# Odd chunks at off-diagonal places of TensorE, in a second PSUM bank, in the triangular inverse and solve of a recurrence

## The chip, the core and the metric

One core of a Trainium2 chip runs the whole program. TensorE (PE) multiplies, with its weight loads shown as a row of their own (PEld); VectorE (DVE), ScalarE (ACT) and GpSimd (POOL) work on elements; SyncE (SP) issues the transfers. The metric is the time of one execution on the device, in microseconds, and the lower the better.

## The reference, cut to what matters

The program computes two blocks one after the other: an attention and mixture-of-experts layer, and then a layer with a convolution, a recurrence and gates. Only the recurrence of the second block is touched. For each of 16 heads of width 64 it runs over 528 positions:

```python
def step(s, inp):
    r_t, w_t, k_t, v_t, a_t, b_t = inp
    sa = jnp.einsum("bhvk,bhk->bhv", s, a_t)
    s = s * w_t[:, :, None, :] + sa[..., None] * b_t[:, :, None, :] + v_t[..., None] * k_t[:, :, None, :]
    y = jnp.einsum("bhvk,bhk->bhv", s, r_t)
    return s, y
```

The kernel does this in chunks of 64 positions. Inside a chunk the steps depend on each other through a strictly triangular 64x64 matrix, so each chunk needs the inverse of (identity minus that matrix), applied to a right-hand side.

## The kernel before

The second block treats two heads at a time: `j` runs from 0 to 7, with head `h` (0 or 1) of the pair in partitions 64h to 64h+63. There are 8 full chunks `c`, and one short one at the start that has its own small tiles (`NX0`, `NT0`). Four stages belong to a `j`: `stage_p` projects (dense products of 24 triples, lines 192 to 194), `stage_x` prepares the chunks, inverts and solves, `stage_y` runs the state over the chunks (line 1532), and beside them `conv_tile` does 30 multiply-adds per tile on DVE (line 1593) and `gate_tile` makes gates from dense products of width 258.

Nobody writes the order of the instructions out by hand. `OFF`, `STEP` and `at` give each stage a priority, and a scheduler lays all instructions of an engine into one list, which the engine then works through in order. So the dense products of lines 192 to 194 (`m` tiles) of another `j`, or of a gate, stand between the steps of the inverse on PE, and the multiply-adds of line 1593 stand between them on DVE. A dense weight tile is split first into two halves, `wh` by ACT (line 160) and `wl` by DVE (line 161), and PE waits for both.

The inverse (lines 1422 to 1438) works on the 32x32 blocks on the diagonal, four for each chunk: quarter `q` of the partitions holds one. The tile `NX` has two planes for each chunk: plane 0 is a power N of the block, plane 1 the running sum X. Five steps `st_` double the power: DVE transposes plane 0 into `NT` (line 1424), PE multiplies `NT` with both planes of `NX` (line 1429), so that N becomes N times N and X gains N times X, DVE adds the old X (line 1435) and ACT copies the new power (line 1437). The first step has plane 0 alone, the last plane 1 alone, so their products are 32 columns wide and those of the three middle steps 64. All are f32, which the trace shows as two records for each product, and each stands at TensorE's place (32q, 32q). The results go to a PSUM tile of the pool `x`, which has two buffers of one bank each (`xps`).

The short chunk does the same in `NX0` (line 1448). Lines 1473 and 1483 join the two 32x32 inverses of a head into a 64x64 one (`X64`), and line 1501 multiplies that with the right-hand side `RT`: 16 products of 64x64 by 64x128, at the places (0, 0) for head 0 and (64, 64) for head 1, chunks 0 to 3 in one bank and 4 to 7 in another. ACT and DVE copy each bank to `LL` (lines 1503 and 1504); line 1512 multiplies `LL` with `QQ` for the tiles `GE` that `stage_y` reads. Those products take their PSUM tile from the same two buffers.

The program below prints these functions with the lines of the profile.

Of the kernel before, what the change touches and what calls it, by code (L numbers as in the profile page):

```python
# [14 lines left out]
AF = mybir.ActivationFunctionType  # L15
OP = mybir.AluOpType
# [75 lines left out]
def tile_blocks(ctx: ExitStack, tc: tile.TileContext, a, out, dbg=None):  # L92
# [30 lines left out]
    x = a["x"][0]  # L123
# [989 lines left out]
    def xps():  # L1113
        return pxy.tile([128, 512], F32, name="x", tag="x", bufs=2)
# [102 lines left out]
    def c4(t):  # L1217
        return t.rearrange("p (c t) -> p c t", c=4)
# [71 lines left out]
    def stage_x(j, z):  # L1290
# [129 lines left out]
        for st_ in range(5):  # L1420
            first, last = st_ == 0, st_ == 4
            w0_, w1_ = int(last), 1 if first else 2
            NT = c8(S2("NT"))
            V.transpose(NT, NX[:, :, 0])
            p = xps().rearrange("p (c w t) -> p c w t", c=8, w=2)
            for c in range(8):
                for q in range(4):
                    qs = slice(32 * q, 32 * q + 32)
                    TE.matmul(p[qs, c, w0_:w1_], NT[qs, c], NX[qs, c, w0_:w1_], start=True, stop=True,
                              tile_position=(32 * q, 32 * q))  # L1430
            nx = UX("NX", "NX", 512, 3).rearrange("p (c w t) -> p c w t", c=8, w=2)
            if first:
                V.tensor_tensor(nx[:, :, 1], NX[:, :, 0], id32[:, None, :].to_broadcast([128, 8, 32]), op=OP.add)
            else:
                V.tensor_tensor(nx[:, :, 1], p[:, :, 1], NX[:, :, 1], op=OP.add)
            if not last:
                A.activation(nx[:, :, 0], p[:, :, 0], AF.Copy)
            NX = nx
        p0 = xps()
        for st_ in range(4):  # L1440
# [52 lines left out]
                      start=True, stop=True, tile_position=(h * 64, h * 64))  # L1493
        for h in range(2):
            A.activation(WV0[:32, h], p[h * 64:h * 64 + 32, 0:64], AF.Copy)
        for i in range(2):
            p = c4(xps())
            for c in range(4):
                for h in range(2):
                    hs = slice(h * 64, (h + 1) * 64)  # L1500
                    TE.matmul(p[hs, c], X64[hs, 4 * i + c], RT[hs, 4 * i + c], start=True, stop=True,
                              tile_position=(h * 64, h * 64))
            A.activation(LL[0:64, 4 * i:4 * i + 4, 0:128], p[0:64], AF.Copy)
            V.tensor_copy(LL[0:64, 4 * i:4 * i + 4, 128:256], p[64:128])

        GE = z.GE = [UX("GE", "GE", 1024, 4).rearrange("p (c h n) -> p c h n", c=4, h=2) for _ in range(2)]
        for i in range(2):
# [396 lines left out]
```

## Time and profile before

| what | value |
|---|---|
| median of three runs | 2100.97 us (2096.94 to 2103.51) |
| the profiled execution | 2105.41 us, its span 2103.6 us |
| mean granted clock of TensorE | 0.979 |
| busy over the span | PE 94%, PEld 79%, DVE 63%, ACT 40%, POOL 2% |
| the second block's loop over `j` | from about 920 to 1455 us of the span |

The profiled execution was 4.4 us slower than the median of the runs shown. The shares of busy time are means over stages that are bound by different things; what counts for this change is the stretch from 920 to 1455 us. A PE record lasts to its modelled end, some 0.2 to 0.3 us after it started, so records overlap and gaps below that length don't show as idle time; the time that a group of products takes is read from its start to the start of what follows it.

### The profile page before, as it was taken

What the parts mean: (1) busy time and instruction counts of PE and PEld (TensorE: products, weight loads), DVE (VectorE), ACT (ScalarE), POOL (GpSimd) and SP (SyncE); (2) the same over time, 40 slices, a digit from 0 to 9 for tenths busy, and PEclk for the clock granted to TensorE, in tenths of its full rate; (3) what the DMA queues carried; (4) which work ended last, traced back from release to release, by engine and by line L of the source; (5) the groups of instructions that cost most, each with busy time, mean ns of one, the idle gap of its engine ahead of it and who ended that gap; (6) DMA issues with size and microseconds to landing.
All of it is one profiled execution on the core that took longest, in us unless ns stands there. A gap on an engine that the chain in (4) does not pass through costs nothing.

```text
span 2103.6 us, 41384 instructions
## 1 busy us (share of the span) xinstructions
PE 1980.9 (94%) x17133; PEld 1672.3 (79%) x17133; DVE 1320.2 (63%) x2919; ACT 832.3 (40%) x1751; POOL 33.9 (2%) x101
## 2 busy tenths in 40 slices
PE   7999999997898999799999999989899999999998
PEld 7778687886454555699888888878799989899997
DVE  4789835443234333679999889886443476455566
ACT  5443544332101111655655656544433253233333
POOL 0000000000000000100000000000000000000000
PEclk9999999998799999999999999999999999999999
DMA  5212021344897997432121112113543323333331
GB/s 160 56 31 82 21 78 44 100 146 154 313 357 301 356 361 273 57 81 58 41 57 57 56 41 59 52 42 103 150 122 94 109 64 91 95 97 91 91 116 51
DMA packets 236964, 247.38 MB, mean 118 GB/s; under 512 B 32156, under 2 KB 190787, under 8 KB 236771
## 3 DMA queue, kind: packets, MB, share of 16 engines
q1 hardware_dynamic: 233315, 234.19, 34.9%
q0 software_dynamic: 2304, 8.39, 1.1%
q8 instruction: 137, 2.24, 0.4%
q10 hardware_dynamic: 1152, 2.10, 0.3%
q14 instruction: 56, 0.46, 0.1%
HBM read 233.79 MB, written 10.84 MB: 116 GB/s over the span
## 4 chain that ended last, share of the span: by engine, by line
PE 68%; issue 13%; DVE 12%; ACT 4%; DMA 2%; POOL 1%; SPq 0%; DVEq 0%; ACTq 0%; POOLq 0%
PE m L194 10%; PE m L192 10%; PE m L193 10%; PE ps L192 5%; PE ps L193 5%; PE ps L194 5%; DVE cv L1593 3%; PE ps L430 2%; PE q L192 2%; PE q L194 2%; DVE wl L161 2%; PE q L193 2%; PE ps L448 1%; PE ps L887 1%; PE y L1532 1%
## 5 line engine op out<-in xcount | busy, mean ns | idle before, releaser
L192 PE MATMUL m<-hh,wh 128*128 128x258 f32 (+1 forms) x1648 | 468.0, 290 | 7.4 <-ACT wh L160 3.0
L194 PE MATMUL m<-hh,wl 128*128 128x258 f32 (+1 forms) x1648 | 466.8, 290 | 2.1 <-DVE wl L161 2.1
L193 PE MATMUL m<-hl,wh 128*128 128x258 f32 (+1 forms) x1648 | 465.7, 288 | 3.0 <-DVE hl L161 1.7
L161 DVE TENSOR_TENSOR wl<-wr,wh 128x1024 fp32r<-128x1024 f32 (+1 forms) x205 | 248.0, 1212 | 228.4 <-ACT wh L160 227.3
L160 ACT ACTIVATE wh<-wr 128x1024 fp32r<-128x1024 f32 (+1 forms) x205 | 214.9, 1050 | 374.4 <-PE m L193 221.3
L192 PEld LDWEIGHTS m<-hh,wh 128*128 128x128 f32 x1648 | 308.4, 189 | 13.9 <-ACT wh L160 3.9
L193 PEld LDWEIGHTS m<-hl,wh 128*128 128x128 f32 x1648 | 308.8, 190 | 7.2 <-DVE hl L161 2.3
L194 PEld LDWEIGHTS m<-hh,wl 128*128 128x128 f32 x1648 | 307.7, 189 | 7.1 <-DVE wl L161 3.3
L1593 DVE SCALAR_TENSOR_TENSOR cv<-th,vec,cv 128x516 f32<-128x516 f32 (+9 forms) x240 | 176.4, 738 | 2.6
L887 PE MATMUL ps<-we,xg 128*64 128x256 f32 x1024 | 135.6, 397 | 5.8 <-PEq L928 5.8
L887 PEld LDWEIGHTS ps<-we,xg 128*64 128x64 f32 x1024 | 76.4, 142 | 53.9 <-issue 21.8
L192 PE MATMUL ps<-wh,hh 128*128 128x256 f32 x352 | 101.7, 289 | 0.9 <-ACT wh L160 0.9
L193 PE MATMUL ps<-wl,hh 128*128 128x256 f32 x352 | 101.2, 288 | 0.7 <-DVE wl L161 0.7
L194 PE MATMUL ps<-wh,hl 128*128 128x256 f32 x352 | 101.0, 287 | 0.0
L192 PEld LDWEIGHTS ps<-wh,hh 128*128 128x128 f32 x352 | 67.4, 191 | 2.0 <-ACT wh L160 1.3
L193 PEld LDWEIGHTS ps<-wl,hh 128*128 128x128 f32 x352 | 67.5, 192 | 1.5 <-DVE wl L161 1.0
L194 PEld LDWEIGHTS ps<-wh,hl 128*128 128x128 f32 x352 | 67.3, 191 | 0.1
L902 PE MATMUL ps<-we,hT 128*64 128x512 f32 x256 | 60.8, 615 | 3.8 <-ACT hT L154 3.3
L1031 PE MATMUL ps<-yph,oht 128*128 128x512 f32 x128 | 56.9, 445 | 6.6 <-DVE x L1033 3.6
L890 ACT ACTIVATE hd<-ps,cw 128x256 f32<-128x256 f32 x16 | 7.6, 474 | 139.6 <-PE ps L887 139.6
L1800 ACT ACTIVATE uu<-m 128x258 f32<-128x258 f32 x88 | 33.1, 378 | 65.6 <-PE m L194 65.6
L192 PE MATMUL q<-wh,zh 128*128 128x512 f32 x144 | 56.7, 396 | 0.4 <-DVE ac L1865 0.2
(554 smaller groups left out, 4201.6 us busy)
## 6 DMA issues: line engine op xcount, KB each, us to landing
wr<-in_w_in_dram SPq DMA_DIRECT2D x94, 512.0 KB
we<-in_w_gate_dram SPq DMA_DIRECT2D x64, 512.0 KB
we<-in_w_up_dram SPq DMA_DIRECT2D x64, 512.0 KB
we<-in_w_down_dram SPq DMA_DIRECT2D x64, 512.0 KB
wr<-in_ffn_up_dram SPq DMA_DIRECT2D x44, 512.0 KB
wr<-in_ffn_down_dram SPq DMA_DIRECT2D x18, 512.0 KB
wr<-in_w_out_dram SPq DMA_DIRECT2D x8, 512.0 KB
wr<-in_w_rwkv_out_dram SPq DMA_DIRECT2D x8, 512.0 KB
```

Of the source, the lines that this page charges most:

```text
L160: A.activation(h, r, AF.Copy)
L161: V.tensor_tensor(l, r, h, op=OP.subtract)
L192: TE.matmul(o, lh, rh, start=start, stop=False)
L193: TE.matmul(o, lh, rl, start=False, stop=False)
L194: TE.matmul(o, ll, rh, start=False, stop=stop)
L430: TE.matmul(ss[r], qf(j)[:, bi * 128:(bi + 1) * 128], kf(j)[:, :nk], start=True, stop=True)
L448: TE.matmul(po[r * 64:(r + 1) * 64, f * 128:(f + 1) * 128], v(kb)[:, j * 64:(j + 1) * 64], ptbs[r][:, kb * 128:(kb + 1) * 128], start=(kb ...
L887: TE.matmul(pg[s * 64:(s + 1) * 64, c0:c0 + 256], XG[k][:, s * 64:(s + 1) * 64], w[s][k], start=(k == 0), stop=(k == 7))
L902: TE.matmul(py[s * 64:(s + 1) * 64], hT[:, f * 128 + s * 64:f * 128 + (s + 1) * 64], wd[s][f][:, hf * 512:(hf + 1) * 512], start=(f == 0), ...
L1031: TE.matmul(p, oht[:, bs], yp[hf][0], start=(i == 0), stop=False)
L1593: V.scalar_tensor_tensor(cv[:, lo:], th[:, lo - d:N2 - d], cdw[:, f, 30 - d:31 - d], cv[:, lo:], op0=OP.mult, op1=OP.add)
L1800: A.activation(t, q, AF.Copy)
```

## The change

In the inverse, each step takes both buffers of the pool `x`, half a bank of each. Even chunks keep the places (32q, 32q) and write to the first. Odd chunks write to the second, and in all steps but the first they stand at places off the diagonal: in steps 1 and 3 rows 32q with columns 32(q+1), so that the result lies one quarter further on, and in steps 2 and 4 rows 32(q+1) with columns 32q, which brings it back. The old X isn't added by DVE any more: a second product for each block, with a 32x32 identity as weights and plane 1 of `NX` as the moving operand, adds it in PSUM (the new line 1435). Then ACT copies the even chunks and DVE the odd ones (new lines 1446 and 1447). In the first step ACT makes two copies instead of one.

In the solve, chunk 2c+i stands at (64h, 64h) for i = 0 and at (64h, 64(1-h)) for i = 1, in the bank of i; the products of both banks take turns, and the copies to `LL` follow for all even chunks and all odd chunks.

```diff
-            p = xps().rearrange("p (c w t) -> p c w t", c=8, w=2)
-            for c in range(8):
-                for q in range(4):
-                    qs = slice(32 * q, 32 * q + 32)
-                    TE.matmul(p[qs, c, w0_:w1_], NT[qs, c], NX[qs, c, w0_:w1_], start=True, stop=True,
-                              tile_position=(32 * q, 32 * q))
+            p = [xps()[:, :256].rearrange("p (c w t) -> p c w t", c=4, w=2) for _ in range(2)]
+            for c in range(0, 8, 2):
+
+                for one in range(1 if first else 2):
+                    for go in range(2):
+                        for q in range(4):
+                            up_ = 0 if first else go
+                            u, o = (q, (q + up_) % 4) if st_ % 2 else ((q + up_) % 4, q)
+                            us, os_ = slice(32 * u, 32 * u + 32), slice(32 * o, 32 * o + 32)
+                            if one:
+                                TE.matmul(p[go][os_, c // 2, 1], id32[us], NX[us, c + go, 1], start=False, stop=True,
+                                          tile_position=(32 * u, 32 * o), skip_group_check=True)
+                            else:
+                                TE.matmul(p[go][os_, c // 2, w0_:w1_], NT[us, c + go], NX[us, c + go, w0_:w1_],
+                                          start=True, stop=first, tile_position=(32 * u, 32 * o), skip_group_check=True)
...
+                A.activation(nx[:, 0::2, 0], p[0][:, :, 0], AF.Copy)
+                A.activation(nx[:, 1::2, 0], p[1][:, :, 0], AF.Copy)
             else:
-                V.tensor_tensor(nx[:, :, 1], p[:, :, 1], NX[:, :, 1], op=OP.add)
-            if not last:
-                A.activation(nx[:, :, 0], p[:, :, 0], AF.Copy)
+                A.activation(nx[:, 0::2, w0_:], p[0][:, :, w0_:], AF.Copy)
+                V.tensor_copy(nx[:, 1::2, w0_:], p[1][:, :, w0_:])
...
+        p = [c4(xps()) for _ in range(2)]
+        for c in range(4):
+            for i in range(2):
+                for h in range(2):
+                    hs, o = slice(h * 64, (h + 1) * 64), 64 * (h ^ i)
+                    TE.matmul(p[i][o:o + 64, c], X64[hs, 2 * c + i], RT[hs, 2 * c + i], start=True, stop=True,
+                              tile_position=(h * 64, o))
         for i in range(2):
-            p = c4(xps())
-            for c in range(4):
-                for h in range(2):
-                    hs = slice(h * 64, (h + 1) * 64)
-                    TE.matmul(p[hs, c], X64[hs, 4 * i + c], RT[hs, 4 * i + c], start=True, stop=True,
-                              tile_position=(h * 64, h * 64))
-            A.activation(LL[0:64, 4 * i:4 * i + 4, 0:128], p[0:64], AF.Copy)
-            V.tensor_copy(LL[0:64, 4 * i:4 * i + 4, 128:256], p[64:128])
+            L_ = LL[0:64, i::2].rearrange("p c (x n) -> p c x n", x=2)
+            A.activation(L_[:, :, i], p[i][0:64], AF.Copy)
+            V.tensor_copy(L_[:, :, 1 - i], p[i][64:128])
```

The lines behind it move down, by 10 after the inverse and by 13 after the solve (1448 is 1458, 1501 is 1512, 1512 is 1525, 1593 is 1606). The scheduler lays the lists out anew. Three places of them follow, before and after.

PE, the last step of the inverse for `j` = 0 and the short chunk's first product behind it; before:

```order
L194 MATMUL m_9822<-hh,wl 128x264
L1429 MATMUL x<-NX,NT 32x32 x32
L1448 MATMUL x<-NX_9350,NT_9548 32x32 x4
L192 MATMUL m_9822<-hh,wh 128x264
L193 MATMUL m_9822<-hl,wh 128x264
L194 MATMUL m_9822<-hh,wl 128x264
```

The same place after, where L1435 is the product with the identity and L1458 the short chunk:

```order
L1438 MATMUL x<-NX,NT 32x32 x8
L1435 MATMUL x<-NX,cst_90 32x32 x8
L1438 MATMUL x<-NX,NT 32x32 x8
L1435 MATMUL x<-NX,cst_90 32x32 x8
L1438 MATMUL x<-NX,NT 32x32 x8
L1435 MATMUL x<-NX,cst_90 32x32 x8
L1438 MATMUL x<-NX,NT 32x32 x8
L1435 MATMUL x<-NX,cst_90 32x32 x8
L192 MATMUL m_9957<-hh,wh 128x264
L193 MATMUL m_9957<-hl,wh 128x264
L1458 MATMUL x<-NX_9350,NT_9683 32x32 x4
L194 MATMUL m_9957<-hh,wl 128x264
```

The step has twice the products, and the short chunk's, which followed at once, now stand apart behind two dense products.

PE, from the solve to the first products with `LL` for `j` = 2; before:

```order
L1501 MATMUL x<-RT,X_11428 64x128 x15
L192 MATMUL m_11765<-hh,wh 128x264
L193 MATMUL m_11765<-hl,wh 128x264
L194 MATMUL m_11765<-hh,wl 128x264
L192 MATMUL m_11765<-hh,wh 128x264
L193 MATMUL m_11765<-hl,wh 128x264
L194 MATMUL m_11765<-hh,wl 128x264
L192 MATMUL m_11765<-hh,wh 128x264
L193 MATMUL m_11765<-hl,wh 128x264
L194 MATMUL m_11765<-hh,wl 128x264
L192 MATMUL m_11765<-hh,wh 128x264
L1512 MATMUL x<-QQ,LL 128x128 x8
```

The same place after (L1512 is now the solve, L1525 the product with `LL`, L1277 and L1278 are dense products of `stage_p`):

```order
L1512 MATMUL x<-RT,X_11833 64x128 x8
L1278 MATMUL m_12245<-low,lwl 128x264
L1277 MATMUL m_12246<-low,lwh 128x264
L1278 MATMUL m_12246<-low,lwl 128x264
L1277 MATMUL m_12247<-loa,lwh 128x264
L1278 MATMUL m_12247<-loa,lwl 128x264
L1525 MATMUL x<-QQ,LL 128x128
L1277 MATMUL m_12248<-loa,lwh 128x264
L1278 MATMUL m_12248<-loa,lwl 128x264
L1525 MATMUL x<-QQ,LL 128x128 x7
```

Five dense products stand between the solve and the first product with `LL` instead of ten, and that product stands alone.

DVE, the inverse for `j` = 7, the last pair of heads, from the second step's addition to the fourth step's; before:

```order
L1435 TENSOR_TENSOR NX<-x,NX 128x8x32
L1593 SCALAR_TENSOR_TENSOR cv<-th,vec_1326,cv 128x516
L1424 STREAM_TRANSPOSE NT<-NX 128x256
L1593 SCALAR_TENSOR_TENSOR cv<-th,vec_1326,cv 128x516
L161 TENSOR_TENSOR wl<-wr,wh 128x1024
L1435 TENSOR_TENSOR NX<-x,NX 128x8x32
L1593 SCALAR_TENSOR_TENSOR cv<-th,vec_1326,cv 128x516
L1424 STREAM_TRANSPOSE NT<-NX 128x256
L1593 SCALAR_TENSOR_TENSOR cv<-th,vec_1326,cv 128x516
L161 TENSOR_TENSOR wl<-wr,wh 128x1024
L1435 TENSOR_TENSOR NX<-x,NX 128x8x32
L1593 SCALAR_TENSOR_TENSOR cv<-th,vec_1326,cv 128x516
```

The same place after, from ahead of the second step's transpose to behind the third step's (L1606 is the multiply-add of `conv_tile`, L1447 the copy of the odd chunks):

```order
L161 TENSOR_TENSOR wl<-wr,wh 128x1024
L1606 SCALAR_TENSOR_TENSOR cv<-th,vec_1326,cv 128x516 x4
L1424 STREAM_TRANSPOSE NT<-NX 128x256
L1606 SCALAR_TENSOR_TENSOR cv<-th,vec_1326,cv 128x516 x3
L1606 SCALAR_TENSOR_TENSOR cv<-th,vec_1326,cv 128x515
L1447 COPY NX<-x 128x4x64
L1606 SCALAR_TENSOR_TENSOR cv<-th,vec_1326,cv 128x514
L1424 STREAM_TRANSPOSE NT<-NX 128x256
L1606 SCALAR_TENSOR_TENSOR cv<-th,vec_1326,cv 128x513
L1606 SCALAR_TENSOR_TENSOR cv<-th,vec_1326,cv 128x512
L1606 SCALAR_TENSOR_TENSOR cv<-th,vec_1326,cv 128x511
L1606 SCALAR_TENSOR_TENSOR cv<-th,vec_1326,cv 128x510
```

Two splits of gate weights (L161) stand inside this piece before; after, the splits stand ahead of the second step or behind the last, and more multiply-adds stand between the steps. The dense products that need the early ones can stand earlier in PE's list between its steps: by the first step's products 35 of width 258 in place of 8, by the last step's 92 in place of 34.

## Rows read from the trace of the kernel before

**Rows 1.** busy time by stretch; columns as headed; `j` = 1 and 7

```profile
core 0: us, PE busy (x) PEld busy (x) DVE busy (x) ACT busy (x) POOL busy (x), PEclk, DMA share, GB/s
984.00:1048.00 64.00, 63.57 (x918) 57.37 (x917) 58.99 (x128) 37.72 (x90) 1.16 (x7) 1.00 0.20 55
...
1378.00:1440.00 62.00, 53.85 (x817) 47.35 (x815) 55.28 (x120) 28.59 (x68) 0.00 (x0) 0.92 0.10 28
```

**Rows 2.** waits, 920 to 1440 us: total us, times, longest us

```profile
PE x L1429 <- DVE NT L1424: 5.0, 11, 1.5
```

**Rows 3.** timeline of PE, the inverse: start us, duration us; [idle before]

```profile
950.12 1.09 PE L1429 MATMUL x<-NX,NT 32*32 32x64 f32 x64
951.15 0.39 PE L193 MATMUL m<-hl,wh 128*128 128x264 f32 x1
...
956.94 0.74 PE L1429 MATMUL x<-NX,NT 32*32 32x32 f32 x64 [0.16 <-DVE NT L1424]
957.53 0.26 PE L1448 MATMUL x<-NX,NT 32*32 32x32 f32 x8
...
1008.84 0.75 PE L1429 MATMUL x<-NX,NT 32*32 32x32 f32 x64
...
1009.52 0.39 PE L194 MATMUL m<-hh,wl 128*128 128x264 f32 x1
```

**Rows 4.** busy time of line 1429 in slices of two steps

```profile
1009.04:1009.14 0.10, 0.10 (x35) 0.10 (x23) 1.00 0.00 0
950.32:950.52 0.20, 0.20 (x28) 0.20 (x22) 1.00 0.00 0
```

**Rows 5.** timeline of PE: products whose places share columns, or rows

```profile
1383.65 1.16 PE L1346 MATMUL x<-ARI,BK 64*128 64x128 f32 x16
1384.74 0.39 PE L192 MATMUL m<-hh,wh 128*128 128x264 f32 x1
...
1401.94 1.15 PE L1399 MATMUL x<-LL,SA 64*64 64x64 f32 x32
1403.02 0.33 PE L1406 MATMUL x<-WV,SC 32*64 32x64 f32 x4
```

**Rows 6.** timeline: solve and first products with `LL`, `j` = 0

```profile
965.55 1.96 PE L1501 MATMUL x<-RT,X 64*64 64x128 f32 x30
966.67 0.59 ACT L1503 ACTIVATE LL<-x 64x512 f32<-64x512 f32 x1 [1.64 <-PE x L1501]
...
967.30 0.69 DVE L1504 COPY LL<-x 64x512 f32<-64x512 f32 x1 [0.71 <-ACT LL L1503]
...
967.44 0.39 PE L192 MATMUL m<-hh,wh 128*128 128x264 f32 x1
...
968.04 1.16 PE L1512 MATMUL x<-QQ,LL 128*128 128x128 f32 x8
...
968.96 0.37 PE L1278 MATMUL m<-low,lwl 128*128 128x264 f32 x1
```

**Rows 7.** groups, 920 to 1440 us: | busy us, mean ns | idle before

```profile
L1512 PE MATMUL x<-QQ,LL 128*128 128x128 f32 x256 | 34.6, 280 | 0.0
...
L1435 DVE TENSOR_TENSOR NX<-x,NX 128x256 f32<-128x256 f32 x32 | 13.4, 419 | 1.3 <-PE x L1429 1.3
...
L1437 ACT ACTIVATE NX<-x 128x256 f32<-128x256 f32 x32 | 12.2, 380 | 34.2 <-DVE NX L1435 30.4 <-PE x L1429 3.8
```

**Rows 8.** busy time around the inverse of `j` = 7; columns as rows 1

```profile
1390.00:1396.00 6.00, 4.66 (x49) 4.01 (x50) 4.59 (x15) 2.49 (x6) 0.00 (x0) 0.72 0.00 0
1396.00:1402.00 6.00, 4.71 (x30) 2.98 (x29) 4.61 (x13) 2.78 (x8) 0.00 (x0) 1.00 0.12 45
1402.00:1408.00 6.00, 3.96 (x164) 3.40 (x164) 6.00 (x10) 2.46 (x6) 0.00 (x0) 0.86 0.02 5
1408.00:1414.00 6.00, 4.47 (x92) 4.16 (x96) 5.70 (x11) 0.77 (x2) 0.00 (x0) 0.57 0.35 95
```

**Rows 9.** timeline of DVE around the inverse of `j` = 7

```profile
1401.04 4.68 DVE L1593 SCALAR_TENSOR_TENSOR cv<-th,vec,cv 128x503 f32<-128x503 f32 x7
```

## The prediction, made before the run

> **What bounds the kernel now.** I read the busy time by stretch first. For a middle pair of heads PE is busy 63.57 of 64 us, DVE 58.99, ACT 37.72, at full clock; the seven pairs `j` = 0 to 6 look alike, and the last, `j` = 7, leaves PE 8 us of 62 and a clock of 0.92 [rows 1]. So for seven pairs PE bounds, and what counts is the time that a piece of PE's list takes. The list of waits says that the transposes hold up PE 5.0 us in all over the eight inverses, 11 times [rows 2]; the dense products between the steps cover the rest of that chain. The timeline of PE then gives the pieces themselves, from the start of one to the start of what follows. A 64-wide step of the inverse takes 951.15 - 950.12 = 1.03 us, a 32-wide one 1009.52 - 1008.84 = 0.68 us, both with 64 records [rows 3]; the next dense product starts some 0.14 us behind the last record (it does so in both: 0.54 us for 63 records at 8.6 ns, 0.89 at 14 ns). These two rates stand in the slices: about 35 records, each some 0.2 us long, touch a slice of 0.1 us of the 32-wide step, which is 0.3 us / 35 = 8.6 ns apiece; 28 touch 0.2 us of the 64-wide one, 0.4 / 28 = 14 ns [rows 4]. The second is the pace at which four places work; the first may be that too (four places, half the columns), but may as well be the pace at which PE takes instructions. This is the question on which the sum turns.
>
> **What the change does to PE, for each `j`.** Removed are no products; each of the four later steps gets 64 more records, the products with the identity.
>
> (a) The three middle steps. If the even and the odd places work side by side, a step of 128 records lasts as long as it takes to feed them: 127 gaps of 8.6 ns are 1.09 us, and with 0.14 behind it is 1.23 us, against 1.03: +0.20 each, +0.60. I take 8.6 ns because it is the fastest sustained rate of small products that a row shows [rows 4]; the bound below is that places alone set the pace (rival B), the bound above that the places take turns (rival C). That places which share rows or columns work side by side is shown for pairs. One place needs 4 x 14 = 56 ns for a record of 64 columns, so 112 for 128. Line 1399, whose two places share their rows, takes 1403.02 - 1401.94 = 1.08 us for 32 records of 64 columns, (1.08 - 0.14) / 32 = 29 ns each, half of 56; line 1346, whose two places share columns and write to two banks, takes 1.09 us for 16 of 128, (1.09 - 0.14) / 16 = 59 ns, half of 112 [rows 5]. No row shows both kinds at once, as here.
>
> (b) The last step has 128 records where it had 64, 32 wide: 1.23 - 0.68 = +0.55 us. The first step keeps 64 records in the same places: 0.
>
> (c) The solve: 30 of its 32 records take 1.89 us [rows 6], of which 0.14 lies behind them. The other 1.75 us are 58 ns a record of 128 columns, two places at work; with four they become half: -0.87 us. The bound above is 0.
>
> (d) The lists are cut into more pieces. The short chunk's first products followed the last step directly (0.59 us after its start, no gap [rows 3]) and now stand alone, and the first product with `LL` stands apart; every switch between small and dense products costs some 0.1 us (the 0.14 of above is of this kind). Two more in a `j`, less what falls away: +0.15 us (0 to 0.35).
>
> (e) A new wait. In before the short chunk's first product took the other PSUM buffer, which was free. Now the last step holds both, so it waits for ACT's copy of the even chunks, with two dense products (0.24 us) in between. ACT's copy took 0.38 us for 256 elements [rows 7]; with half of them I take 0.27, and with some 0.4 us for results to land and two handovers 0.67 us from the last even product, of which 0.34 is covered: +0.3 us (0 to 0.6; all dense products of PE's list queue behind that product).
>
> (f) A second wait, at the first product with `LL`. In before the first bank's copies ran during the second half of the solve (ACT started at 966.67, DVE ended at 967.99, the products started at 968.04 [rows 6]), and PE waited 0.0 us there [rows 7]. Now both banks end together. From the last record of the solve, some 0.2 us to land, 0.59 for ACT's and 0.69 for DVE's copy side by side, handovers: 1.1 us to the first, and the second pair of copies 0.7 later, 1.85 us to where DVE's odd copy is done, 1.65 counted from the first dense product. Between stand 5 to 15 dense products (9, 10, 5, 10, 12, 15, 11, 10 for the eight `j`) of 0.12 us, 0.6 to 1.8 us. So the wait is 0 to 0.9 us; I take +0.5. DVE's copies stand behind a multiply-add of 0.67 us [rows 9] at times, which is why I don't take less.
>
> Per `j`: 0.60 + 0.55 - 0.87 + 0.15 + 0.3 + 0.5 = +1.23 us, times 8 = +9.8 us.
>
> **What lies off PE.** DVE loses an addition of 0.42 us and gets a copy of as many elements, 0.42 again [rows 7], in the last step half of it; ACT no longer waits for DVE's addition (30.4 us of its idle time [rows 7], which cost nothing, since ACT is busy 60%). The copies of a step are now side by side, each waiting for PE alone, so `NT` comes somewhat earlier: of the 5.0 us of rows 2 I take back 1.5 (0 to 5).
>
> **The last pair.** From 1390 to 1414 us PE is busy 17.8 of 24, and the granted clock is 0.72, 1.00, 0.86 and 0.57 [rows 8]; the clock fell after PE had stood idle in parts. Here the list of PE had no gate products to put between the steps; now 92 stand ahead of the last step's end instead of 34, 58 x 0.118 = 6.8 us of work. Against it: DVE's list has five multiply-adds, a copy and a transpose between two transposes there, 5 x 0.67 + 0.3 + 0.38 = 4.0 us [rows 7, 9], and PE's steps with 15 dense products need 1.23 + 1.8 = 3.0. PE would still wait 1 us in three steps. So -4 us (0 to -6.8).
>
> **A rule against the change.** Rows 4 show a small record every 8.6 ns. The Trainium skill, page "TensorEngine Tiling (Array Packing)", section "Performance Considerations", puts some 60 cycles on every matmul however narrow, and advises against gaining places from a dimension that is already small; at 2.4 GHz that would be 25 ns for each of 64 added records, an estimate of 1.6 us a step and 51 us in all. The trace disagrees: 64 records took 0.68 us [rows 3].
>
> **Sum.** +9.8 - 1.5 - 4 = +4.3 us on the profiled 2105.41: 2109.7. That execution was 4.4 us above the median of 2100.97, so the forecast is **2105 us**.
>
> **Rivals.** B: PE takes instructions faster than 8.6 ns, and the places set the pace. With eight places at work instead of four, the 64 records of 64 columns need half of 0.89 us and the 64 with the identity half of 0.54: with the 0.14 behind them 0.86 us for a middle step (-0.17), and 0.68 as before for the last. Per `j` that is -0.51 - 0.87 + 0.95 = -0.43, in all -3.4 - 5.5 = -8.9 us: 2092 us. For it: the 8.6 ns is close to a quarter of a place's 32 ns, so it may be no limit of the feed. Against it: no row shows a faster rate held over a whole step. This is also what the span model of the Trainium skill ("TensorE: Matmul & The Clock Gate", section "Measured speedup vs the span model") would make of it, which adds only some 4 ns for each place. Chance 0.15.
>
> C: the change doesn't do what it says; off-diagonal places wait for those of the diagonal. Then a middle step is 0.89 + 0.54 + 0.14 = 1.57 us (+0.54), the last 1.23, the solve gains nothing: 1.62 + 0.55 + 0.95 = +3.1 per `j`, 25 - 5.5 = +19: 2120 us. Rows 5 speak against it. Chance 0.08.
>
> D, slower: the copies that now come after both banks. If ACT or DVE is still in other work when the products end (a multiply-add of 0.67 us, a split of a weight tile), e and f cost their full 0.6 and 0.9, and `j` = 7 gains nothing since DVE sets the pace there: 0.60 + 0.55 - 0.87 + 0.35 + 1.5 = 2.13 per `j`, 17 - 1.5 = +15.5: 2116 us. It decides where fewer than some 16 dense products stand ahead of the first product with `LL`, which is so in every `j`; for it DVE's 92% of busy time, against it that PE's feed goes on while copies run. Chance 0.17.
>
> E: the waits e and f are hidden (f has 1.8 us of dense products at best) and the last pair gains all of 6.8 us: per `j` 0.28 + 0.1, 3.0 - 1.5 - 6.8 = -5.3: 2096 us. Chance 0.17.
>
> **How the numbers follow.** My forecast, A, has 0.43. About 0.3% (6.3 us) is what a measurement of this kernel can tell from no change: below 2094.7 it is faster, above 2107.3 slower. Faster: B 0.14, half of E 0.08, A's edge 0.02, together 0.24. Slower: C 0.08, D 0.16, a fifth of A 0.09, together 0.33. The same: 0.43. The range from 2091 to 2117 leaves out half of B, C, and a part of D, some 0.2.
>
> **What would show it.** In the trace of after: the start of a middle step to the next dense product 1.23 us (0.86 by B, 1.57 by C), the last step's likewise, the solve's 32 records in 0.9 us (1.74 by C); idle time of PE at the short chunk's first product with ACT's copy as releaser (e) and at the first product with `LL` (f), some 2 and 4 us in all; and PE's busy time between 1390 and 1414 us, 2 to 4 us more, with the clock nearer to 1. I would be wrong if the scheduler's new list moves a wait into stages that I didn't look at.

## The result: 1.5% slower

The changed kernel takes 2132.52 us (median of four runs, 2130.58 to 2140.03) beside 2101.01 before: a ratio of 1.0145 with an interval of 1.0126 to 1.0164, 31 us slower. The forecast was 2105, the range ended at 2117. In the profiled execution the span is 2128.8 us instead of 2103.6.

The rows of after that answer to [rows 1] are these (us of the stretch, busy time and count of PE, PEld, DVE, ACT and POOL, granted clock, share of the DMA engines, GB/s):

```profile
984.00:1048.00 64.00, 59.56 (x1124) 53.40 (x1123) 56.00 (x120) 33.93 (x80) 1.06 (x6) 0.97 0.20 55
...
1378.00:1440.00 62.00, 59.24 (x953) 53.27 (x956) 56.19 (x119) 32.61 (x79) 0.93 (x4) 0.98 0.16 45
1440.00:1500.00 60.00, 55.29 (x687) 50.12 (x679) 27.92 (x58) 25.46 (x57) 0.00 (x0) 0.88 0.32 91
```

PE has a fifth more records between 984 and 1048 us, and is idle 4.4 us there in place of 0.4. The list of waits (us in total, times, longest) says for what:

```profile
PE x L1438 <- DVE NT L1424: 10.4, 15, 0.9
...
PE x L1435 <- issue: 5.3, 5, 1.8
PE x L1438 <- issue: 2.7, 2, 2.0
PE x L1458 <- issue: 1.9, 2, 1.7
```

The transposes hold PE up 10.4 us, where it was 5.0 [rows 2]. The other three are new, but for one such wait in before:

```profile
PE x L1429 <- issue: 0.8, 1, 0.8
```

PE stands still for up to 2 us in the middle of the inverse, at lines 1438, 1435 and 1458 (the short chunk), and "issue" says that it waits for nothing that the profile shows.

To see where all 25 us went, I added up, from the trace, the time from the start of each PE product to the start of the next, by the kind of both, from the last product of the first block's line 1031 to the first of line 1788 (1801 in after). This is a sum over 9,579 records of products in before and 11,627 in after, and loses nothing. us:

```
                                          before    after   change
records inside steps (gaps up to 0.24)      31.8     43.5    +11.7
gaps over 0.24 inside the inverse            4.1     10.6     +6.5
dense product to the next step              12.3     20.2     +7.8
to the short chunk, and its long gaps        5.4     11.3     +5.9
solve                                       14.8     10.5     -4.3
dense product to products with LL            1.6      3.6     +1.9
other small products of the recurrence     115.5    111.0     -4.5
dense to dense                             500.1    501.9     +1.8
all                                        841.4    869.3    +27.9
```

(The rest, switches between the kinds above all, is 155.8 and 156.9 us. The blocks ahead of it, which the change doesn't touch, happened to be 3.2 us shorter in the profiled execution.) Of the 4.1 us of before, 3.0 are waits between steps of `j` = 7 that follow each other directly; in the middle of a step PE stood still only once, for 1.04 us. In after it does so eleven times.

### The profile page after: what moved, and what is told of

Read it like the earlier page. It is cut to its first block, busy times and chain, and to the rows that moved or that the text cites. A ratio compares the mean times of both kernels' runs of the same rounds, so it can differ in the third digit from the quotient of the medians.

```text
span 2128.8 us, 45529 instructions
## 1 busy us (share of the span) xinstructions
PE 1995.9 (94%) x19181; PEld 1684.9 (79%) x19181; DVE 1324.2 (62%) x2919; ACT 833.8 (39%) x1767; POOL 33.8 (2%) x101
## 5 line engine op out<-in xcount | busy, mean ns | idle before, releaser
L193 PE MATMUL m<-hl,wh 128*128 128x258 f32 (+1 forms) x1648 | 470.8, 291 | 2.3 <-DVE hl L161 1.4
L161 DVE TENSOR_TENSOR wl<-wr,wh 128x1024 fp32r<-128x1024 f32 (+1 forms) x205 | 248.3, 1212 | 230.5 <-ACT wh L160 227.7
L192 PEld LDWEIGHTS m<-hh,wh 128*128 128x128 f32 x1648 | 310.2, 191 | 10.2 <-ACT wh L160 3.6
L1606 DVE SCALAR_TENSOR_TENSOR cv<-th,vec,cv 128x516 f32<-128x516 f32 (+9 forms) x240 | 177.7, 740 | 3.9
L887 PEld LDWEIGHTS ps<-we,xg 128*64 128x64 f32 x1024 | 76.3, 142 | 53.9 <-issue 21.4
L1438 PE MATMUL x<-NX,NT 32*32 32x64 f32 (+1 forms) x2560 | 49.1, 215 | 13.2 <-DVE NT L1424 10.4
```

Of the source, the lines that this page charges most:

```text
L161: V.tensor_tensor(l, r, h, op=OP.subtract)
L192: TE.matmul(o, lh, rh, start=start, stop=False)
L193: TE.matmul(o, lh, rl, start=False, stop=False)
L887: TE.matmul(pg[s * 64:(s + 1) * 64, c0:c0 + 256], XG[k][:, s * 64:(s + 1) * 64], w[s][k], start=(k == 0), stop=(k == 7))
L1438: TE.matmul(p[go][os_, c // 2, w0_:w1_], NT[us, c + go], NX[us, c + go, w0_:w1_], start=True, stop=first, tile_position=(32 * u, 32 * o), ...
L1606: V.scalar_tensor_tensor(cv[:, lo:], th[:, lo - d:N2 - d], cdw[:, f, 30 - d:31 - d], cv[:, lo:], op0=OP.mult, op1=OP.add)
```

## What brings PE to a stop in the middle of a step

One of the eleven, in the timeline of PE of after (start, duration, engine, line, count, idle time before):

```profile
1089.62 0.24 PE L1435 MATMUL x<-NX,cst 32*32 32x32 f32 x5
1090.95 0.26 PE L1435 MATMUL x<-NX,cst 32*32 32x32 f32 x6 [1.10 <-issue]
1091.14 0.39 PE L193 MATMUL m<-hl,wh 128*128 128x264 f32 x1
```

Five records of the last products of a step start, then nothing for 1.29 us, then the remaining six. No operand is missing in between: all of them need the same tiles. The only thing that the DMA engines do at that time is in the transfers of the stretch 1088.7 to 1089.9 us (queue and kind: packets, MB, share):

```profile
q8 instruction: 1, 0.02, 5.0%
```

A packet of 16,384 bytes of instructions starts at 1088.80 and ends at 1089.76, and PE goes on 1.19 us later. The page of each kernel shows whose instructions these are. First before, then after:

```profile
PE 1980.9 (94%) x17133; PEld 1672.3 (79%) x17133; DVE 1320.2 (63%) x2919; ACT 832.3 (40%) x1751; POOL 33.9 (2%) x101
...
q8 instruction: 137, 2.24, 0.4%
```

```profile
PE 1995.9 (94%) x19181; PEld 1684.9 (79%) x19181; DVE 1324.2 (62%) x2919; ACT 833.8 (39%) x1767; POOL 33.8 (2%) x101
...
q8 instruction: 153, 2.51, 0.5%
```

2048 more records of products and 2048 more of weight loads go with 16 more packets: 16 x 16,384 / 4096 = 64 bytes a record, 256 records a packet. A step of the changed inverse has 128 records of products and 128 of loads. It uses up a whole packet in 1.2 to 1.35 us, while a dense product and its load use up two records in 0.12 us, 15 us a packet. The ten longest stops inside steps, with the packet before each, from the trace:

```
packet ends    PE goes on    after     stop
 947.52         949.00       1.48      0.80
1009.75        1011.18       1.42      0.25
1089.76        1090.95       1.19      1.29
1154.53        1155.92       1.40      1.04
1159.92        1161.31       1.39      2.17
1163.30        1164.79       1.48      0.29
1166.74        1168.26       1.52      0.32
1291.13        1292.61       1.47      0.99
1373.54        1374.92       1.39      1.15
1434.39        1435.87       1.49      2.03
```

In all ten PE goes on 1.2 to 1.5 us after a packet has ended. There is a sharper sign in the trace: PE stops at the same place of a packet each time. Ahead of the first product after the stop shown above PE has worked through 8,159 records of products, as many loads and 177 other instructions (semaphores for the most part), 16,495 in all, which is 64 x 256 + 111. For all eleven stops inside steps, and the two in the short chunk, the remainder is 111 or 112. So it is for all 73 waits in the inverse and the short chunk that the traces of before, after and the twelve kernels below put down to "issue". The two long waits for a transpose in before have 31 and 159.

So theory F: steps of 128 records drain what PE holds of its own list, and PE then stands still until the next packet has been brought and taken over. Theory W set against it: the new waits (for the transposes, for the copies of two banks) are what costs. Theory S: it is the solve.

## Experiments

**One part at a time.** The first kernel has the inverse as changed and the solve as before, the second the reverse.

> The inverse as changed, the solve as before. Theory F (the step's doubled records, and the bringing in of PE's instructions, which cannot keep up with them): the whole loss lies in the inverse, and the solve had given some 4 us back, so 2130 to 2140 us, with PE standing still inside steps for about 11 us in all, each time until some 1.4 us after the end of a packet of instructions. Theory S (the second bank of the solve and its late copies cost the most): 2110 us or less.

> The solve as changed, the inverse as before. Theory F: a small gain, 2096 to 2102 us: the solve's records take half (about -0.6 us for each pair of heads) and the first products with LL wait some 0.3 us more. Theory S: 2112 us or more.

The inverse alone: 2137.31 us, 1.0176 (1.0148 to 1.0205). The solve alone: 2105.41, 1.0018 (1.0006 to 1.0030). S falls. The small gain that F expected of the solve (2096 to 2102 us) did not come either. In the solve alone, the 240 gaps inside the solve fell from 14.8 to 7.9 us, -0.86 us for each `j`, and the time ahead of the products with `LL` rose from 1.6 to 5.1. The total stops inside steps with the inverse alone were 7.1 us, fewer than the 11 expected; the waits for the transposes were 11.4.

**Fewer instructions, same sums.** The product with the identity has the same weights for all chunks, so one product can move four chunks of a place:

```diff
+            for go in range(0 if first else 2):
+                for q in range(4):
...
+                    TE.matmul(p[go][os_, :, 1], id32[us], NX[us, go::2, 1], start=False, stop=True,
+                              tile_position=(32 * u, 32 * o), skip_group_check=True)
```

Of this there are three forms. In the first every product with `NT` starts a sum, as in the changed kernel, so that the old X is added for the last chunk of a place only and overwrites elsewhere; the number of products is the same as in the third. In the second it stands ahead, starts the sum, and the others add. In the third it stands behind, and only chunk 0 and 1 start a sum (`start=first or c == 0`).

> All of the change, but one product with the identity for the four chunks of a place instead of four: 8 in a step in place of 32, each with 128 columns, so 80 records in a step in place of 128. Theory F: stalls inside steps fall to under 4 us in all, a middle step takes about 0.85 us, the time is 2090 to 2104 us. Theory W (the new waits: for the transposes, and for the copies of two banks) expects those waits to stay: 2115 to 2125 us.

> One product with the identity for the four chunks of a place, issued ahead of the products with NT, which add to it; 80 records in a step, the rest as changed. Theory F alone: stalls inside steps 2 us or less, a middle step about 0.85 us, 2092 to 2102 us. Theory W (DVE's queue of multiply-adds ahead of the copy and the transpose): PE waits some 12 to 15 us for the transposes, as the steps are shorter than what stands in DVE's list between them, and the time is within 0.3% of before.

> One product with the identity for the four chunks of a place, behind the products with NT, the first of which alone clears the sums of the bank; 80 records in a step. The list of instructions is that of the kernel with one product behind (2103 us), so 2099 to 2107 us. If what the products add to matters for the pace, another time.

The first took 2102.96 us, 0.9992 (0.9971 to 1.0014), the third 2103.14, 1.0000 (0.9987 to 1.0013): taking 48 of the 128 records out of a step gives back the whole loss. In the third the gaps over 0.24 us inside the inverse are 0.9 us (10.6 in after), a middle step lasts 1.07 us, and the sum over the second block is 840.6 (841.4 in before). The waits for the transposes did not go down with it. The third form's list:

```profile
PE x L1432 <- DVE NT L1424: 14.6, 23, 1.2
...
PE x L1438 <- issue: 0.6, 1, 0.6
```

That is 14.6 us where after has 10.4 (14.7 in the first form). W expected these waits to stay, and with them 2115 to 2125 us; they stayed, and the time was that of before. So they aren't what separates after from these kernels. The step was longer than the 0.85 us of the expectation: 80 records at 11 ns, and 0.2 us behind the wide products. The form with the product ahead took 2119.33, 1.0072 (1.0058 to 1.0087), slower than either theory expected, and its list has no wait for `NT` at all. A product that doesn't wait for `NT` is set earlier by the scheduler and then stands apart: 94 switches from dense products to the inverse and back, where the others have 40, 9 us more than in the third on the way back, of the 19 us by which the sum over its block is longer.

An intermediate number of records, 96 in a step:

> As the kernel with one product with the identity behind, but one for two chunks: 16 in a step, 96 records. Theory F (the feed of instructions): stalls inside steps between those of 80 records (1 us) and of 128 (11 us), 2 to 5 us in all; a middle step about 1.1 us. If the stalls came from something other than the number of instructions, they stay where either neighbour has them.

One execution: 2107.53 us, a middle step of 1.19 us, gaps over 0.24 us inside the inverse 1.6 us in all, a little under what F expected, and 14.0 us of waits for the transposes. With 64, 80, 96 and 128 records the stops are 1.0 (in before, without the waits of `j` = 7), 0.9, 1.6 and 10.6 us. They don't grow evenly with the number of records: most of them begin between 96 and 128.

**Same instructions, fewer columns.** The product with the identity moves one column in place of 32:

```diff
-                                TE.matmul(p[go][os_, c // 2, 1], id32[us], NX[us, c + go, 1], start=False, stop=True,
+                                TE.matmul(p[go][os_, c // 2, 1, 0:1], id32[us], NX[us, c + go, 1, 0:1], start=False, stop=True,
```

> All of the change, but each product with the identity moves one column instead of 32 (the rest of the old X is left out). The number of instructions stays. If the feed of instructions bounds the step (theory F), a middle step stays at 1.2 us or more and the stalls inside steps stay at 7 to 12 us: 2120 to 2133 us. If the columns at the places bound it, a middle step falls to 0.9 us and the stalls with it: below 2115 us.

One execution: 2117.35 us, between the two. But the rows decide for F: records inside steps 43.4 us as in after (43.5), an undisturbed middle step 1.33 us (1.35), stops inside the inverse 10.0 us (10.6). The list of waits:

```profile
PE x L1435 <- issue: 5.4, 7, 1.7
PE x L1438 <- DVE NT L1424: 3.3, 9, 0.5
PE x L1438 <- issue: 1.9, 5, 0.5
```

The columns of the products with the identity cost nothing; their number does. What this kernel saves against after is for the most part in the waits for the transposes, 3.3 us instead of 10.4.

**No product with the identity.** DVE adds the old X, at off-diagonal places and in two banks. Here the old X of odd chunks isn't moved along with the places, which is left out.

```diff
...
-                A.activation(nx[:, 0::2, w0_:], p[0][:, :, w0_:], AF.Copy)
-                V.tensor_copy(nx[:, 1::2, w0_:], p[1][:, :, w0_:])
+                for go in range(2):
+                    V.tensor_tensor(nx[:, go::2, 1], p[go][:, :, 1], NX[:, go::2, 1], op=OP.add)
+            if not first and not last:
+                for go in range(2):
+                    A.activation(nx[:, go::2, 0], p[go][:, :, 0], AF.Copy)
```

> All of the change without products with the identity: off-diagonal places and two banks stay, the old X is added by DVE, in two additions of 128 elements a partition in place of one of 256. Theory F: 64 records in a step again, at eight places, about 0.70 us for a middle step, no more stalls inside steps than in before (1 us), the time 2088 to 2100 us. Theory W: the two banks are held longer by DVE's additions and PE waits for the transposes as much as in after: 2112 us or more.

2108.76 us, 1.0029 (1.0019 to 1.0040): neither. The steps do nearly what F expects. A middle step, from its start to the next dense product, in the timeline of PE:

```profile
1003.43 0.85 PE L1432 MATMUL x<-NX,NT 32*32 32x64 f32 x64
1004.22 0.39 PE L192 MATMUL m<-hh,wh 128*128 128x264 f32 x1
```

0.79 us in place of 1.03 [rows 3]: 10.2 ns a record at eight places, 14 at four (F had expected 0.70 us). So off-diagonal places do work beside the diagonal ones; that it isn't the second bank shows in the next kernel, which keeps it. In all the inverse's records took 24.7 us in place of 31.8 and the stops 0.3. But these 7 us did not reach the end: ahead of the steps 16.2 us in place of 12.3, ahead of the short chunk 8.0 in place of 5.4, and the other small products of the recurrence 123.3 in place of 115.5. Which of them would have come without the change of places isn't settled.

**All at diagonal places.** The changed kernel, with odd chunks on the diagonal (`up_ = 0`).

> All of the change, with its products with the identity, but odd chunks at the diagonal places too (second bank kept). If the off-diagonal places work side by side with the diagonal ones, four places now take turns at 128 records: 0.89 + 0.54 + 0.14 = 1.57 us for a middle step instead of 1.35, the last step 1.22 as before (its pace is that of the feed), so about 8 x 3 x 0.2 = 5 us slower than the changed kernel, less what covers waits: 2133 to 2140 us. If the off-diagonal places give nothing, 2130 to 2134 us and a middle step of 1.35.

2129.77 us, 1.0114 (1.0096 to 1.0132), just under what was expected if the off-diagonal places gave nothing, and no slower than the changed kernel. But the step says that they give something: a middle step lasts 1.53 us (1.57 expected), 0.18 more than in after, 4.3 us for 24 of them. The gain by places is real in the step and can't be seen in the whole; the waits and stops are less here: 18.3 us ahead of the steps (20.2 in after), 8.3 of stops (10.6).

**The waits for the transposes.** What stands in DVE's list between two transposes? Before, a step of `j` = 1:

```profile
1013.60 0.44 DVE L1424 STREAM_TRANSPOSE NT<-NX 128x256 f32<-128x256 f32 x1
1013.96 0.71 DVE L1593 SCALAR_TENSOR_TENSOR cv<-th,vec,cv 128x516 f32<-128x516 f32 x1
...
1014.59 0.49 DVE L1173 SCALAR_TENSOR_TENSOR lp<-m,vec,lq 128x264 f32<-128x264 f32 x1
1015.00 0.75 DVE L1593 SCALAR_TENSOR_TENSOR cv<-th,vec,cv 128x516 f32<-128x516 f32 x1
...
1015.66 0.42 DVE L1435 TENSOR_TENSOR NX<-x,NX 128x256 f32<-128x256 f32 x1
1016.00 0.75 DVE L1593 SCALAR_TENSOR_TENSOR cv<-th,vec,cv 128x516 f32<-128x516 f32 x1
...
1016.66 0.44 DVE L1424 STREAM_TRANSPOSE NT<-NX 128x256 f32<-128x256 f32 x1
```

After, the same step:

```profile
1014.18 0.44 DVE L1424 STREAM_TRANSPOSE NT<-NX 128x256 f32<-128x256 f32 x1
1014.54 1.18 DVE L161 TENSOR_TENSOR wl<-wr,wh 128x1024 fp32r<-128x1024 f32 x1
1015.65 0.48 DVE L1173 SCALAR_TENSOR_TENSOR lp<-m,vec,lq 128x264 f32<-128x264 f32 x1
1016.05 1.54 DVE L1606 SCALAR_TENSOR_TENSOR cv<-th,vec,cv 128x516 f32<-128x516 f32 x2
1017.50 0.42 DVE L1447 COPY NX<-x 128x256 f32<-128x256 f32 x1
1017.83 0.75 DVE L1606 SCALAR_TENSOR_TENSOR cv<-th,vec,cv 128x514 f32<-128x514 f32 x1
1018.50 0.44 DVE L1424 STREAM_TRANSPOSE NT<-NX 128x256 f32<-128x256 f32 x1
```

DVE is never idle in either, but the distance is 4.3 us in place of 3.1. The products of this step ended at 1016.0 and the copy came at 1017.50, behind two multiply-adds. From the second transpose of an inverse to the last there stand 3.3 multiply-adds on average between two of them before, 4.25 in after and 3.7 with one product behind. That the scheduler had planned the step longer than it is would explain it, but no run shows that.

To see whether that makes the time, I took the copy off DVE, on top of the form with the product ahead, and then cut half of the multiply-adds (15 of 30 for each tile) out of both kernels.

```diff
-                V.tensor_copy(nx[:, 1::2, w0_:], p[1][:, :, w0_:])
+                A.activation(nx[:, 1::2, w0_:], p[1][:, :, w0_:], AF.Copy)
```

> As the kernel with one product with the identity ahead, and ACT copies both banks, so that only the transpose is left to DVE in a step: three multiply-adds instead of four and a copy between two transposes. Theory W: PE's waits for the transposes fall from 12 to 15 us to under 7, the time to 2088 to 2098 us. Against it: ACT's two copies come one after the other, 0.4 us later than side by side; if that sets the step, the waits stay (with ACT as the releaser) and the time is 2100 us or more.

```diff
-            for d in range(1, 31):
+            for d in range(1, 16):
```

> The kernel before with 15 of the 30 multiply-adds of each tile of the convolution left out, so that DVE has some 10 us less to do for each pair of heads. If PE alone bounds the stretch, the time stays within 0.5% of before; where PE's waits for the transposes (5 us) go, 2 to 5 us less: 2094 to 2100 us.

> The changed kernel with the same 15 multiply-adds left out. Theory W (the multiply-adds that stand in DVE's list ahead of the copy and the transpose make PE wait): in the steps that have four or five of them between two transposes PE still waits 0.7 to 1.0 us, in those that have none it doesn't wait, and the distance to the same cut of the kernel before falls from 31 to about 25 us. Theory F alone: the distance stays at 28 us or more.

With both copies on ACT: 2139.94 us, 1.0170 (1.0143 to 1.0197). W's price can't be read from it: the kernel that it builds on had no wait for the transposes to lose, and here the wait is 2.0 us. The time rose by 21 us against that kernel; in three stretches of some 66 us the granted clock was 0.93, 0.86 and 0.82, and PE waited for weight halves (5.4 us for `wl`, 4.3 for `wh`; 2.0 and 2.4 in that kernel).

Half of the multiply-adds: the kernel before 2116.90 us, 1.0069 (1.0054 to 1.0084), the changed one 2159.49, 1.0272 (1.0256 to 1.0287). Less work for DVE made both slower, which no theory expected, and the distance, which W saw at 25 us and F at 28 or more, grew from 31 to 43. What happens within the steps of the cut kernel is plain, though. DVE, in the cut of the changed kernel:

```profile
1015.08 0.44 DVE L1424 STREAM_TRANSPOSE NT<-NX 128x256 f32<-128x256 f32 x1
1015.44 3.08 DVE L1606 SCALAR_TENSOR_TENSOR cv<-th,vec,cv 128x516 f32<-128x516 f32 x4
1018.44 0.42 DVE L1447 COPY NX<-x 128x256 f32<-128x256 f32 x1
...
1019.43 0.44 DVE L1424 STREAM_TRANSPOSE NT<-NX 128x256 f32<-128x256 f32 x1
1019.80 0.45 DVE L1173 SCALAR_TENSOR_TENSOR lp<-m,vec,lq 128x264 f32<-128x264 f32 x1
1021.46 0.42 DVE L1447 COPY NX<-x 128x256 f32<-128x256 f32 x1 [1.22 <-PE x L1435]
1021.99 0.45 DVE L1424 STREAM_TRANSPOSE NT<-NX 128x256 f32<-128x256 f32 x1
```

And PE, in the step that the last of these transposes releases:

```profile
1023.65 0.23 PE L1438 MATMUL x<-NX,NT 32*32 32x32 f32 x5 [0.81 <-issue]
```

Behind five multiply-adds and the copy the next step (at 1019.93 us) starts 1.19 us after the dense product ahead of it, which is a wait of 1.0. Behind none there is no wait (0.21 us), and PE stands still inside that step. So it goes on: the gaps over 0.24 us inside the inverse rose to 19.1 us, while the waits for the transposes fell to 7.5. Here the two causes stand in for each other. While PE waits for a transpose its list can be filled up; where steps follow each other more closely, it runs dry more often. The steps of 128 records bear this out: of those that start 0.6 us or more after the product ahead of them, 2 of 14 have a stop in after (2 of 11 in this kernel), of the others 9 of 18 (16 of 21). It isn't a rule that a wait less is a stop more: with one column moved the waits fell by 7.1 us at the same stops. The rest of the distance, 12 us between dense products (519.1 and 506.6), goes with a granted clock of 0.87, 0.96, 0.91 and 0.83 in four stretches of the cut changed kernel; why the clock fell there is open. Why the cut kernel before lost 13 us is open too; its list has PE waiting 7.9 us for `wl` between 920 and 1500 us, 2.1 in before.

## Why the prediction was wrong, step by step

- **"PE bounds" for seven pairs, and the pace is the question.** Right as a question. The answer, 8.6 ns a record, held for the last step: 1.22 us where it ran undisturbed (1.23 forecast). A middle step took 1.35 us, 9.7 ns a record, not 1.23. One column in place of 32 leaves the 9.7, so the columns of the products with the identity aren't what holds it, and rival B (0.86 us) is out. The products of 64 columns may hold part of it: by themselves they took 10.2 ns a record at eight places. This is 0.12 x 24 = 3 us more than (a).
- **The step that failed** is that the feed was taken for a rate alone. A rate held over 64 records was carried over to 128, as if the supply behind it had no end. The supply comes in packets of 256 records, and stops of 0.25 to 2.2 us in the middle of a step made 10.6 us, where before had 1.0. Together with (a) and (b) the records cost 11.7 us and the stops 9.5, 21 us against 9 that the forecast had.
- **What lies off PE.** The forecast took back 1.5 us of the waits for the transposes, since the two copies stand side by side. They do, but the new list puts a multiply-add more between two transposes; the waits became 10.4 us. I had read DVE's new list for `j` = 7 alone, where five multiply-adds stand between two transposes; it is longer for the other seven pairs as well. That sign was wrong, by 7 us. What these waits cost by themselves is open: with one product behind they were 14.6 us, and the time was that of before.
- **(c) the solve.** -0.87 us forecast, -0.86 measured in the solve alone. In after the sum is -4.3 and not -6.9: half of the difference comes at `j` = 7, where PE ran at a granted clock of 0.50 from 1454 to 1460 us, the rest at four other pairs, where the solve took 1.20 to 1.64 us instead of 0.99.
- **(d) the pieces.** In the second block's loop PE's list goes from dense products to others 285 times in place of 259, three more for each pair and not two. What a switch costs was not measured apart.
- **(e) the wait of the short chunk.** Forecast 2.4 us for ACT's copy. The time ahead of the short chunk rose by 3.6 us, and 2.3 more inside it, but of PE's idle time there 1.9 us is "issue" and 0.2 ACT:

```profile
L1458 PE MATMUL x<-NX,NT 32*32 32x32 f32 (+1 forms) x256 | 9.9, 217 | 2.7 <-issue 1.9 <-DVE NT L1454 0.3 <-ACT NX L1446 0.2
```

  About the size, by other causes: there are 32 switches from dense products to these in place of 24, of 0.2 to 0.5 us each, and the 2.3 us inside are two stops after the last step, when the list has just been drained.
- **(f) the wait for `LL`.** Forecast 4 us; measured 1.9 ahead of the products, and 1.8 at the switches behind them. Idle time had been 0.0 [rows 7]; DVE's copy of `LL` is now the releaser named, once, for 1.1 us. Right in place, half in size.
- **The last pair.** Right in the idle time, wrong in the time. The rows of 1378 to 1440 us above look like the gain (59.2 us busy and not 53.9, the clock 0.98 and not 0.92 [rows 1]), but the inverse of `j` = 7 now runs from 1426 to 1444 us, not from 1404 to 1417. From the first product of line 1346 for `j` = 7 to the first of line 1622 (1635 in after) PE is idle 8.6 us in place of 12.8, the 4 us that were forecast; yet this stretch lasts 113.5 us in place of 110.5. The granted clock is still low in it: 0.92, 0.79, 0.78 and 0.50 from 1432 to 1456 us, in steps of 6 us.
- **C** is out (10.2 ns a record at eight places without products with the identity). **D**, the slower rival, put its loss into (e) and (f) and ended at 2116, 16 us short. What it named, DVE still in a multiply-add when the products end, is seen ahead of the transposes instead, and `j` = 7 gained nothing, as it said. **E** is out: (f) wasn't hidden, and `j` = 7 gained nothing.
- The time of a record in an undisturbed step of after was 8.6 to 9.7 ns, 17 to 19 for a product of two records. The rule of the Trainium skill that the prediction weighed ("TensorEngine Tiling (Array Packing)", section "Performance Considerations": some 60 cycles for every matmul, by the prediction's estimate 25 ns) isn't borne out by it, and of the stops it doesn't speak.

## What to carry to other kernels

Count the instructions of a burst, not only their pace: here PE's list came in packets of 256 records, and bursts of 256 within 1.2 to 1.35 us, weight loads counted, stopped PE for up to 2.2 us at a time and 10.6 us in all, while those of 160 or 192 hardly did (0.9 and 1.6 us in all). A matrix added by products with the identity costs by their number: with 8 wide products in place of 32 narrow ones the time was back at that of before, which is no gain over the addition by DVE either. And where a scheduler fills the time between two links of a chain, a change of the chain changes the filling (3.3 multiply-adds between two transposes became 4.25): read the list of every engine in the chain at an ordinary place, not only at the end of the program.

## What the runs showed of the hardware

- A packet of 16 KB of PE's instructions takes about 1 us to come (0.96 for the one above). Where PE had run dry it went on 1.2 to 1.5 us after a packet's end, and each time it had stopped at the same place of a packet, number 111 or 112 of 256.
- Eight 32x32 places, four on the diagonal and four off it, in two banks, took 10.2 ns a record of 64 columns, four took 14: 1.4 times the rate, not twice. With 32 columns the eight places took 8.9 ns in most last steps of the same kernel, and the four of before 8.8: no gain. With the identity among them, in after, it was 8.6.
- Why the first form with one product behind adds the old X for the last chunk of a place only, and why in the third form the products of later chunks need no start, no row shows by itself. The Trainium skill, page "PSUM — Partial Sum Buffer", section "Terms", states it: a product that starts a sum clears the marks of what has been written in the whole bank for the groups of 32 partitions that it writes, and a product without a start adds where a mark is set and overwrites where none is. Both forms agree with it.
